# Low parts of w_down's weights: a ScalarE rounding with scale -1 and an accumulating DMA in place of VectorE's subtraction

## The chip, the cores and the metric

The kernel runs on one core of one Trainium2 chip. The metric is device microseconds of one execution: 2164.78 us in the median of 3 runs before the change (2164.6 to 2165.61).

## The reference, cut to what matters

Two layers of a streaming encoder are computed for a prompt of 512 frames and a sample of 64 frames with the same weights. Each layer has three kinds of attention over one combined projection, and then a gated feed-forward part:

```
xn = rmsnorm(x);  g, u = split(xn @ w_up)          # D_MODEL 1024, D_FF 2816
h  = gelu(causal_dwconv3(g)) * u
x  = x + h @ w_down                                # w_down: 2816 x 1024
```

All is float32. The kernel gets float32-like accuracy out of matmuls on operands of the shorter type fp32r: each factor is split into `hi` (the value rounded to fp32r) and `lo` (what the rounding left), and a product is the sum of three matmuls, hi\*hi, hi\*lo and lo\*hi. The change is about how `lo` of w_down's weights is made.

## The kernel before, in words

**Tokens.** Prompt and sample are handled together as 576 columns, in two halves of 288 (`halves`, L69), with the feature dimension on the partitions.

**Chunks.** All weights go through one list of *chunks* (`chunk`, L368), each of 128 rows by up to 1024 columns of float32 in SBUF. A chunk of w_in, w_up or w_out has eight k-tiles and one block of 128 output columns; a chunk of w_down has four k-tiles (two in the first group) and two column blocks (`ncol=2`). The main loop (`run_main`, L424) takes them in order. At the start of chunk i it asks for the weights of chunk i+2 (`fetch`, L375, a DMA from SP into `raw`, three buffers) and makes the generator `split(i + 1)` (L385) the first entry, label "w", of the list of pending steps. For each column block and each half it then issues the chunk's matmuls, k-tile by k-tile, in the order hi\*hi, hi\*lo, lo\*hi: the third matmul of a chunk is the first that reads `lo`. The results go to PSUM tiles from a pool of two (`pmm`); after each group VectorE adds or multiplies them out (`flush`, L411).

**split.** ScalarE rounds the two halves of `raw` to `hi`, and VectorE subtracts `hi` from `raw` to make `lo` (L400 to L406). `hi` and `lo` have two buffers each, so the tiles for chunk i+1 come free when PE has finished chunk i-1, which is the start of chunk i.

**Order.** There are no hand-written queues: a planner in the program (`charge`, `tick`) keeps a model clock for PE, ScalarE, VectorE and GpSimd, and lets each pending generator take its next step after every three matmuls, when the model says that its inputs are ready. "w" steps are first in the list and have no other condition. Each engine then runs what it got in that order. Only instructions issued through the wrapped engines (`scalar`, `vector`, `gpsimd`) are charged to the model clocks.

**Feed-forward part.** The 22 column blocks of w_up are taken in six groups (`FG`, L42: 2, 4, 4, 4, 4, 4). Block f has a gate chunk `g` (`evg`, L1247) and an up chunk `u` (`evu`, L1275), then `fin` (L1278): GpSimd multiplies `ge` by `ur`, ScalarE rounds the product to `hh`, VectorE subtracts to get `hl`. A group's part of w_down is a run of four chunks d0 to d3 (`down`, L1312); their evacuation (L1316) is VectorE's add of the PSUM tile `md` into `x`. The run for a group stands behind the `g` and `u` chunks of the next group's first block (of its last block for the last group), so `fin` of that block falls into the run's first chunk. In layer 0 the run of the last group follows directly and also starts the next norm for each finished tile (`norm_tile`, L507: ScalarE's `xhm` and square, VectorE's `xlm`, GpSimd's sum `accm`). In layer 1 the last group goes another way (`down_final`, L1327), with `half` set; it keeps the split as it was.

Of the kernel before, what the change touches and what calls it, by code (L numbers as in the profile page):

```python
# [13 lines left out]
AF = mybir.ActivationFunctionType  # L14
ALU = mybir.AluOpType
# [30 lines left out]
def trunk_kernel(ctx: ExitStack, tc: tile.TileContext, a: dict, o: dict):  # L46
    nc = tc.nc
# [15 lines left out]
    def slot(nm, dt=F32):  # L63
        return sp_.tile([P, TOK], dt, tag="s", name=nm, bufs=NS)
# [59 lines left out]
    scalar = Engine(nc.scalar, "ACT", act_cost)  # L124
# [260 lines left out]
    def split(i):  # L385

        c = chunks[i]
        if "hi" in c:
            return
        c["hi"] = None  # L390
        n = c["kt"] // 2
        raw = c["raw"]
        if c["half"] is None:
            hi, lo = (wp.tile(c["shape"], F32R, tag=f"w{t}", name=f"w{t}{c['nm']}", bufs=2) for t in ("hi", "lo"))
            hi, lo = ([t[:, 0:n, :], t[:, n:2 * n, :]] for t in (hi, lo))
        else:
            hi, lo = ([slot(f"w{t}{j}{c['nm']}", F32R)[:, 0:512].rearrange("p (k c) -> p k c", k=n)
                       for j in range(2)] for t in ("hi", "lo"))
        ks = slice(0, n), slice(n, 2 * n)
        scalar.copy(hi[0], raw[:, ks[0], :])  # L400
        t0 = cx["t"]
        scalar.copy(hi[1], raw[:, ks[1], :])
        cx["t"] = t0
        yield
        for j in range(2):
            vector.tensor_tensor(lo[j], raw[:, ks[j], :], hi[j].bitcast(F32), op=ALU.subtract)  # L406
        c["hi"], c["lo"] = ([t[k // n][:, k % n, :] for k in range(2 * n)] for t in (hi, lo))
# [16 lines left out]
    def run_main(start):  # L424
        for i in range(start, len(chunks)):
# [5 lines left out]
            if i + 1 < len(chunks):  # L431
                spawn("w", split(i + 1), True)
# [1146 lines left out]
    def split_first(i):  # L1579

        if i == 2:
            list(split(2))
            return w0.append((chunks[2]["hi"], chunks[2]["lo"]))
        raw = chunks[i]["raw"]
        hi, lo = ([slot(f"w{n}{i}{j}", F32R)[:, 0:512].rearrange("p (k c) -> p k c", c=P) for j in range(2)]
                  for n in "hl")
        for j in range(2):
            scalar.copy(hi[j], raw[:, 4 * j:4 * j + 4, :])
        for j in range(2):
            vector.tensor_tensor(lo[j], raw[:, 4 * j:4 * j + 4, :], hi[j].bitcast(F32), op=ALU.subtract)  # L1590
        w0.append(tuple([t[k // 4][:, k % 4, :] for k in range(ND)] for t in (hi, lo)))
        chunks[i]["raw"] = None
# [42 lines left out]
    for d in range(4, ND):  # L1635
        if d + 2 < ND:
            rows(d + 2)()
            square(d + 1)
        if d == 5:
            square(ND - 1)  # L1640
        if d == 6:
            list(split(3))
        for i in range(3):
            if d == 6 and i == 1:
                norm_end("m0")
            grow(i, d)
# [71 lines left out]
```

## Time and profile before

| | |
|---|---|
| median of 3 runs | 2164.78 us |
| the profiled execution's own time | 2164.78 us |
| its span, first to last instruction | 2163.0 us |
| PE matmul busy | 2135.8 us, 99% of the span |
| VectorE (DVE) busy | 1393.0 us, 64% |
| ScalarE (ACT) busy | 1041.3 us, 48% |
| GpSimd (POOL) busy | 398.1 us, 18% |
| 16 DMA engines, share taken by the SP queue | 30.6% |

How to read the rows: a timeline row is start in us, duration in us (of all the instructions that it merges), engine, line, operation, output and inputs, shape and count, and in brackets how long the engine was idle before it and for whom it waited. All instructions issued through the wrapped engines have line L102, so tiles tell them apart: `whid` and `wlod` are the hi and lo parts of a w_down chunk, `wrd` its raw weights. A waits row is who waited for whom: us in total, times, longest. A chain row is start, us, what. A grouped row ends in busy us, mean ns of one, and the idle time before. A DMA row ends in KB each and us from issue to landing, where that is known.

### The profile page before, as it was taken

The numbers are of one execution on the slowest core, as the hardware profiler recorded it, in microseconds if no ns is written. First come the engines' busy times: TensorE is split into PE (matmuls) and PEld (weight loads), VectorE is DVE, ScalarE is ACT, GpSimd is POOL, SyncE is SP. The second block draws the span as 40 slices with busy tenths as digits, with TensorE's granted clock in tenths as the row PEclk, the third lists the DMA queues.
The fourth block names the chain that finished last, engine by engine and source line by source line (L and its number), as shares of the span: only waits on it lengthen the run. The fifth ranks groups of instructions, "written<-read, shape, count | busy, mean of one in ns | idle before, by whom it ended". The sixth has DMA issues, their size and how long they took to land.

```text
span 2163.0 us, 39766 instructions
## 1 busy us (share of the span) xinstructions
PE 2135.8 (99%) x15911; PEld 2099.8 (97%) x15911; DVE 1393.0 (64%) x2860; ACT 1041.3 (48%) x2057; POOL 398.1 (18%) x523
## 2 busy tenths in 40 slices
PE   8999999999999999999999999999999999999998
PEld 7999999999999999999999999999999999999998
DVE  7886667767466655556678765667765566555564
ACT  5657776555434322323355677755554333222334
POOL 2111121111122111212110122201102112111221
PEclk9999999999999999999999999999999999999999
DMA  7442222223332322222243222233323322222222
GB/s 216 122 139 84 73 85 80 89 79 97 93 118 60 101 84 82 85 79 88 88 139 107 83 73 73 73 93 98 99 74 122 88 79 81 86 78 88 78 89 65
DMA packets 326563, 200.50 MB, mean 93 GB/s; under 512 B 10544, under 2 KB 320754, under 8 KB 326314
## 3 DMA queue, kind: packets, MB, share of 16 engines
q1 hardware_dynamic: 324618, 194.88, 30.6%
q0 software_dynamic: 1760, 3.08, 0.4%
q8 instruction: 125, 2.05, 0.4%
q14 instruction: 60, 0.49, 0.1%
HBM read 176.54 MB, written 25.83 MB: 94 GB/s over the span
## 4 chain that ended last, share of the span: by engine, by line
PE 92%; DVE 5%; issue 1%; ACT 1%; POOL 1%; DMA 0%; SPq 0%; DVEq 0%; POOLq 0%; ACTq 0%
PE md L131 11%; PE mg1f L131 6%; PE mg0f L131 6%; PE mu0f L131 6%; PE mu1f L131 6%; PE mo L131 4%; PE mg0a L131 2%; PE mg1a L131 2%; PE mg0b L131 2%; PE mg1b L131 2%; PE mg0c L131 2%; PE mg1c L131 2%; DVE wlod L102 1%; PE mb1a L131 1%; PE mb0a L131 1%
## 5 line engine op out<-in xcount | busy, mean ns | idle before, releaser
L102 DVE TENSOR_TENSOR x<-md,x 128x288 f32<-128x288 f32 x192 | 86.9, 455 | 117.2 <-PE md L131 116.3
L102 ACT CAST whid<-wrd 128x512 fp32r<-128x512 f32 (+1 forms) x88 | 46.8, 579 | 138.1 <-PE md L131 87.9
L131 PE MATMUL md<-hh0f,whid 128*128 128x288 f32 x352 | 104.9, 298 | 3.5 <-DVE x L102 3.5
L131 PE MATMUL mu0f<-xhf,wlou0f 128*128 128x288 f32 x352 | 103.8, 295 | 0.0
L131 PE MATMUL mu1f<-xhf,wlou1f 128*128 128x288 f32 x352 | 103.8, 295 | 0.0
L131 PE MATMUL md<-hh0f,wlod 128*128 128x288 f32 x352 | 103.8, 295 | 0.0
L131 PE MATMUL mg1f<-xhf,whig1f 128*128 128x288 f32 x352 | 103.7, 295 | 0.0
L131 PE MATMUL mg0f<-xhf,whig0f 128*128 128x288 f32 x352 | 103.7, 295 | 0.0
L131 PE MATMUL mg0f<-xhf,wlog0f 128*128 128x288 f32 x352 | 103.7, 295 | 0.0
L131 PE MATMUL mg1f<-xhf,wlog1f 128*128 128x288 f32 x352 | 103.7, 295 | 0.0
L131 PE MATMUL mu1f<-xlf,whiu1f 128*128 128x288 f32 x352 | 103.7, 295 | 0.0
L131 PE MATMUL mu0f<-xlf,whiu0f 128*128 128x288 f32 x352 | 103.7, 295 | 0.0
L131 PE MATMUL mu0f<-xhf,whiu0f 128*128 128x288 f32 x352 | 103.6, 294 | 0.0
L131 PE MATMUL mu1f<-xhf,whiu1f 128*128 128x288 f32 x352 | 103.6, 294 | 0.0
L131 PE MATMUL md<-hl0f,whid 128*128 128x288 f32 x352 | 103.6, 294 | 0.0
L131 PE MATMUL mg0f<-xlf,whig0f 128*128 128x288 f32 x352 | 103.6, 294 | 0.0
L131 PE MATMUL mg1f<-xlf,whig1f 128*128 128x288 f32 x352 | 103.6, 294 | 0.0
L131 PE MATMUL md<-hh1f,whid 128*128 128x288 f32 x288 | 85.7, 297 | 2.7 <-DVE x L102 2.7
L131 PE MATMUL md<-hh1f,wlod 128*128 128x288 f32 x288 | 84.9, 295 | 0.0
L131 PE MATMUL md<-hl1f,whid 128*128 128x288 f32 x288 | 84.8, 294 | 0.0
L131 PE MATMUL mo<-ml,whio 128*128 128x288 f32 x256 | 75.6, 295 | 0.8 <-DVE ml L102 0.8
L131 PE MATMUL mo<-mh,wloo 128*128 128x288 f32 x256 | 75.5, 295 | 0.0
(960 smaller groups left out, 8434.1 us busy)
## 6 DMA issues: line engine op xcount, KB each, us to landing
wrd<-in_w_down SPq DMA_DIRECT2D x40, 512.0 KB
wrg0f<-in_w_up SPq DMA_DIRECT2D x22, 512.0 KB
wru0f<-in_w_up SPq DMA_DIRECT2D x22, 512.0 KB
wrg1f<-in_w_up SPq DMA_DIRECT2D x22, 512.0 KB
wru1f<-in_w_up SPq DMA_DIRECT2D x22, 512.0 KB
wro<-in_w_out SPq DMA_DIRECT2D x16, 512.0 KB
xspill<-x SPq DMA_DIRECT2D x16, 288.0 KB
x<-xspill SPq DMA_DIRECT2D x16, 288.0 KB
```

The lines of the kernel that those rows point to most:

```text
L102: return f(*args, **kw)
L131: nc.tensor.matmul(out, lhsT=lhsT, rhs=rhs, start=start, stop=stop, skip_group_check=True)
```

## The change

For w_down chunks that have no `half`, ScalarE makes two more instructions: it writes the negated rounding of `raw` into the `lo` tile (a Copy with scale -1, output fp32r). Then one DMA issued from GpSimd adds `raw` into that tile (SBUF to SBUF, accumulating). VectorE's two subtractions of the chunk are gone, and `split` is done in one planner step, in which the DMA is charged to no model clock.

```diff
         if c["half"] is None:
             hi, lo = (wp.tile(c["shape"], F32R, tag=f"w{t}", name=f"w{t}{c['nm']}", bufs=2) for t in ("hi", "lo"))
+            c["lo_t"] = lo
             hi, lo = ([t[:, 0:n, :], t[:, n:2 * n, :]] for t in (hi, lo))
...
         scalar.copy(hi[0], raw[:, ks[0], :])
         t0 = cx["t"]
         scalar.copy(hi[1], raw[:, ks[1], :])
+        if c["nm"][0] == "d" and c["half"] is None:
+
+            for j in range(2):
+                scalar.activation(lo[j], raw[:, ks[j], :], AF.Copy, scale=-1.0)
+            nc.gpsimd.dma_start(c["lo_t"][:, 0:2 * n, :], raw, accum_op=ALU.add)
+            c["hi"], c["lo"] = ([t[k // n][:, k % n, :] for k in range(2 * n)] for t in (hi, lo))
+            yield
+            return
         cx["t"] = t0
         yield
         for j in range(2):
             vector.tensor_tensor(lo[j], raw[:, ks[j], :], hi[j].bitcast(F32), op=ALU.subtract)
```

## Rows read from the trace of the kernel before

**Rows 1.** The page: busy us, share of the span and instructions of each engine.
```profile
PE 2135.8 (99%) x15911; PEld 2099.8 (97%) x15911; DVE 1393.0 (64%) x2860; ACT 1041.3 (48%) x2057; POOL 398.1 (18%) x523
```
**Rows 2.** PE's waits over the whole span.
```profile
PE md L131 <- DVE x L102: 6.2, 15, 0.7
```
**Rows 3.** PE's waits in the stretches 690:760, 760:1040 and 1040:1095.
```profile
PE md L131 <- DVE x L102: 1.2, 2, 0.7
...
PE md L131 <- DVE x L102: 1.5, 4, 0.4
...
PE md L131 <- DVE x L102: 0.8, 3, 0.3
```
**Rows 4.** The chain that ended last, 744 to 800 us.
```profile
745.58 6.36 PE mu0f L131 x48
```
**Rows 5.** Timeline of PE, first matmul of a w_down run.
```profile
764.50 0.29 PE L131 MATMUL md<-hh0f,whid 128*128 128x288 f32 x1
```
**Rows 6.** Timeline of ScalarE: short run, ordinary run, layer 0's last run.
```profile
698.65 0.71 ACT L102 CAST whid<-wrd 128x256 fp32r<-128x256 f32 x2 [2.32 <-issue]
...
764.61 1.14 ACT L102 CAST whid<-wrd 128x512 fp32r<-128x512 f32 x2 [1.97 <-issue]
767.27 0.67 ACT L102 CAST hh0f<-ge0f 128x576 fp32r<-128x576 f32 x1 [1.52 <-POOL ge0f L102]
...
1067.93 1.12 ACT L102 CAST whid<-wrd 128x512 fp32r<-128x512 f32 x2
```
**Rows 7.** Timeline of VectorE: short run's end, ordinary run's start, layer 0's last run.
```profile
711.02 1.28 DVE L102 TENSOR_TENSOR wlog0f<-wrg0f,whig0f 128x512 fp32r<-128x512 f32 x2
...
765.26 2.53 DVE L102 TENSOR_TENSOR wlod<-wrd,whid 128x512 fp32r<-128x512 f32 x2
...
768.08 0.75 DVE L102 TENSOR_TENSOR hl0f<-ge0f,hh0f 128x576 fp32r<-128x576 f32 x1
768.74 0.45 DVE L102 TENSOR_TENSOR x<-md,x 128x288 f32<-128x288 f32 x1
...
1066.18 0.46 DVE L102 TENSOR_TENSOR x<-md,x 128x288 f32<-128x288 f32 x1 [0.68 <-PE md L131]
```
**Rows 8.** Timeline of GpSimd: short run's first chunk, ordinary run's first chunk.
```profile
699.38 1.43 POOL L102 TENSOR_TENSOR ge0f<-ge0f,ur0f 128x576 f32<-128x576 f32 x1 [6.15 <-ACT whid L102]
...
765.33 1.91 POOL L102 TENSOR_TENSOR ge0f<-ge0f,ur0f 128x576 f32<-128x576 f32 x1 [5.73 <-ACT whid L102]
```
**Rows 9.** Timeline of SP's queue in the same chunk.
```profile
767.82 0.37 SPq L383 DMA_DIRECT2D wrg0f<-in_w_up  x1
```
**Rows 10.** Groups by form, VectorE's subtractions for w_down.
```profile
L102 DVE TENSOR_TENSOR wlod<-wrd,whid 128x512 fp32r<-128x512 f32 x72 | 58.1, 849 | 2.4
L102 DVE TENSOR_TENSOR wlod<-wrd,whid 128x256 fp32r<-128x256 f32 x16 | 7.5, 512 | 0.0
```
**Rows 11.** Groups by form, ScalarE's casts and activations of 128x512.
```profile
L102 ACT CAST whid<-wrd 128x512 fp32r<-128x512 f32 x72 | 41.1, 618 | 119.4 <-PE md L131 79.8 <-issue 15.7 <-PE mg0f L131 11.9
...
L102 ACT ACTIVATE ge0f<-c0f 128x512 f32<-128x512 f32 x22 | 13.5, 615 | 0.0
```
**Rows 12.** DMA queues, and issues from GpSimd with KB and us to landing.
```profile
q1 hardware_dynamic: 324618, 194.88, 30.6%
...
ewin<-ebias POOLq DMA_DIRECT2D x1, 1536.0 KB, 12.8
...
out_sa_k<-in_cache_a_k POOLq DMA_DIRECT2D x2, 128.0 KB, 3.2
out_sa_v<-in_cache_a_v POOLq DMA_DIRECT2D x2, 128.0 KB, 4.4
```
**Rows 13.** Groups of GpSimd: what its DMA issues take of the engine.
```profile
L291 POOL DMA_DIRECT2D ewin<-ebias x2 | 2.3, 1133 | 11.0 <-DMA ebias<-ev 11.0
...
L363 POOL DMA_DIRECT2D out_sa_v<-in_cache_a_v x2 | 1.0, 498 | 0.0
```
**Rows 14.** Cores: span and mean granted clock.
```profile
core 0: 2163.0 us, clock 0.999
```

## The prediction

> **What bounds the kernel now.** I read the busy table first: PE is busy for 2135.8 of 2163.0 us and VectorE for 64% [rows 1]. So at most 27 us of PE's idle time could be won anywhere, and VectorE's load matters only where PE waits for it. The list of PE's waits puts a price on that: the w_down matmuls (tile `md`) wait 15 times for VectorE's add into `x`, 6.2 us in all [rows 2]. That is the ceiling of what taking work off VectorE here can return. By stretch it is 1.2 us around each layer's first, short w_down run (layer 1's line reads the same), 1.5 us in four waits, one for each ordinary run of layer 0, and 0.8 us in its last run [rows 3]; what is left for layer 1's ordinary runs is 6.2 - 2 x 1.2 - 1.5 - 0.8 = 1.5 us. Then I read how long a chunk lasts: 48 matmuls take 6.36 us of PE time, whether eight k-tiles by one column block or four by two [rows 4]. A first-group chunk (two k-tiles, 24 matmuls) is 3.18 us. Last I read, engine by engine, one chunk start and what hangs on it [rows 5 to 9].
>
> Call the start of a chunk T. In the run at 764.50 [rows 5], ScalarE begins to round the next chunk's weights at 764.61, when PE lets go of the two-deep `hi` buffer, and two casts take 1.14 us [rows 6]. VectorE's two subtractions follow at 765.26 and take 2.53 us [rows 7], so low parts that PE needs at T+6.36 are ready at T+3.3: three microseconds to spare.
>
> **The change, part by part.**
>
> *How often.* Only w_down chunks with no `half` are touched: the trace has 72 subtractions of 128x512 and 16 of 128x256 [rows 10], two a chunk, so 36 long chunks and 8 short ones, in runs of four: 9 long runs and 2 short ones. One long run is layer 0's last; the other eight and both short ones stand right behind an `up` chunk whose `fin` step (GpSimd's product, ScalarE's rounding to `hh`, VectorE's `hl`) shares the start of the run.
>
> *ScalarE.* Two more instructions a chunk. The trace has no Copy with a scale and no pointer here; the cast of 128x512 is 618 ns and the 128x512 activation 615 ns [rows 11], and pairs go through in 1.14 us, so I take 0.55 us more each: four end at T+2.3, in a short chunk (a pair is 0.71 us [rows 6]) at T+1.45. ScalarE is 48% busy, so the time itself is covered; only the chain counts.
>
> *VectorE.* 58.1 + 7.5 us of subtractions go [rows 10]. Off the path, but for the waits of rows 3. Of those 6.2 us I count back the eight of the ordinary runs (3.0), layer 0's last (0.8) and 0.5 at each short run's start, 4.8 us. The 0.7 at each short run's end follows the subtraction for the next gate chunk (711.02 [rows 7]), which stays.
>
> *The accumulating DMA.* No row shows one. From below: the quickest GpSimd DMA of the trace takes 3.2 us from issue to landing for 128 KB; from above: 12.8 us for 1536 KB [rows 12]. Between them: the SP queue's 194.88 MB held 30.6% of 16 engines [rows 12], 10590 engine-us over the span, so 512 KB needs 1.8 us of all sixteen and 128 KB 0.45. That makes 3.2 - 0.45 + 1.8 = 4.55 us for a copy, and 6.35 if reading the old value doubles the traffic. I take the middle, L = 5.5 us for 512 KB and 4.1 for 256 KB (issue and wake-up included), nearer the 128 KB row because it too stands alone on its queue; I keep 3.2 and 12.8 as ends.
>
> The Trainium skill ("DMA: Bandwidth & Descriptors", Anatomy of one DMA) gives 2.0 us plus bytes over 436 GB/s: by that 512 KB would land after an estimated 3.2 us. The trace's 128 KB DMAs took 3.2 and 4.4 us where that formula says 2.3. The skill's "Collectives: The Full Stack" (Part 3, why ReduceScatter is half of AllGather) says an add inside the DMA halves the rate because two sources are read; no run here shows it. Together they would make an estimated 4.4 us, and the sum below about 2183 us.
>
> *What the landing costs PE.* The low part is wanted by the third matmul, so weights must be there by T + 6.36 + 0.15 = T+6.5; they land at T+2.3+L. First chunk of a long run: 2.3+5.5-6.5 = 1.3 us late. The second chunk's chain starts when the first chunk starts, before that stall, so the stall is given back to it and it is on time; the third is late by 1.3 again, the fourth is not. L below 4.2 costs nothing. In a short run the chunk ahead is 3.18 us: need at T+3.3, landing at T+1.45+4.1 = 5.55, so second and fourth chunk are 2.2 us late each (the first follows a long chunk, need T+6.5, on time): 4.4 a run, 8.8 for two.
>
> *What is queued behind the DMA.* GpSimd is in order, and the DMA is emitted at the first planner step of a chunk, `fin`'s product at a later one. The product now starts at 765.33 = T+0.8 [rows 8]; it will wait for the fourth rounding (T+2.3) and for the issue (1.1 us, by the ewin issue's 1133 ns; the 64-row issues are 0.5 [rows 13]): T+3.45. Without the subtraction beside it, it runs 1.43 us, as at 699.38, not 1.91 [rows 8], to T+4.9. Then `hh` 0.67 (T+5.6) and `hl` 0.75 (T+6.35), and `hl` stands in VectorE's order ahead of the second add into `x` (768.08 before 768.74 [rows 7]). That add ends at T+6.8, but the fourth PSUM group of the chunk, which reuses its bank, wants to begin at T+4.77: PE waits 2.0 us. It overlaps the landing's 1.3 (both end at fixed times after T), so the first chunk costs 2.0, not 3.3. In short runs the same chain ends at T+6.0, inside the landing stall.
>
> *Layer 0's last run* has no `fin`, but its `xhm` and squares stand ahead of the roundings: the third chunk's first cast begins at 1067.93, while the add at 1066.18 shows its predecessor's start to be 1065.98 [rows 6, 7], so its chain is 1.9 us later than elsewhere. Cost: 1.3 at its first chunk, 2.3+1.9+5.5-6.5 = 3.2 at its third: 4.5.
>
> *SP's queue.* A weight fetch into the buffer that the DMA reads now waits for the landing (T+7.8) and not for the subtraction (767.82 = T+3.3 [rows 9]). That buffer is wanted for the rounding that starts three chunks on, at T+19, 11 us after the landing. The fetch is hidden behind those chunks and costs nothing; if that cover were gone, ScalarE's rounding, and with it the whole chain, would start later by what the fetch is late.
>
> *Clock.* 0.999 granted over the span [rows 14]; I count nothing for it, as the stalls are short.
>
> *Sum.* 8 x (2.0+1.3) + 4.5 + 8.8 - 4.8 = 26.4 + 4.5 + 8.8 - 4.8 = +34.9 us. The profiled execution took 2164.78 us, 1.8 more than its span and equal to the median of the runs: 2164.8 + 34.9 = 2199.7, say 2200 us.
>
> **Rivals.**
>
> *A, the transfer is hidden.* If L is 3.2 us (the 128 KB row taken as it stands; the DMA formula of the Trainium skill says the same), no long chunk waits for its landing. What is left: the product behind the DMA, 8 x 2.0; short runs 4 x (1.45+3.2-3.3) = 5.4; last run 0.9; less 4.8: +17.5, 2182 us. For it: the path is SBUF to SBUF. Against: four times the bytes and an add.
>
> *B, the transfer is slow.* With L = 8.5 (between 6.35 and the 12.8 row; other DMAs on the same engines, or a slower add): 4.3 late at two chunks of each long run, 8 x 8.6 = 69, last run 10.5, short runs 2 x 10.5, less 4.8: +95, 2260 us. At L = 12.8 it would be about +195. For it: the kernel's own fetches use the same engines. Against: they hold them for only 30.6%.
>
> *C, faster.* `fin`'s chain does not block: if the planner, with VectorE no longer charged, sets `hl` behind the second add, or the product ahead of the DMA, and L is under 4.2 us, then nothing is late in the long runs and the waits of rows 3 go: -4.8 in the ideal case, 2160 us. It decides where the product starts before T+1.6 or `hl` loses its place. Against: `split` is first in the list of steps, and the product's place depends on PE's and ScalarE's model clocks, which change little.
>
> **Numbers.** Forecast 0.50, A 0.19, B 0.22, C 0.05, no change to speak of 0.04. Predicted time 2200. The range runs from a little below A, 2176, to L = 8, 2250. A measurement of this kernel tells about 0.2%, 4.3 us, from no change: faster 0.05, same 0.04, slower 0.91; all of the forecast, A and B are slower.
>
> **What would show it.** In the profile after, PE's waits name the DMA into `wlod` (1 to 2 us, first and third chunk of long runs, second and fourth of short ones) and VectorE's `x` with about 2 us once in each run behind `fin`; GpSimd's product starts 2.6 us later in those chunks and lasts 1.4; VectorE loses some 65 us and ScalarE gains some 45. I am wrong if the DMA lands under 4 or over 8 us after its issue, if stalls come in every chunk and not every other, or if `hl` stands elsewhere.

## The result, and the profile after

The kernel after takes 2189.52 us in the median of 3 runs (2187.12 to 2189.56), the kernel before 2164.78: ratio 1.011, interval 1.0087 to 1.0133. That is 24.7 us slower, inside the range on record (2176 to 2250) and 10.5 us under the predicted 2200. The profiled execution's span grew from 2163.0 to 2187.3 us.

The page's first part answers to [rows 1]: VectorE has 62 us less, ScalarE 43 us more, and PE is busy 8.6 us longer for the same 15911 matmuls.

```profile
PE 2144.4 (98%) x15911; PEld 2105.2 (96%) x15911; DVE 1331.1 (61%) x2772; ACT 1084.3 (50%) x2145; POOL 425.1 (19%) x567
```

PE's waits over the whole span answer to [rows 2]. The adds into `x` went from 6.2 to 1.5 us, and a wait for the DMA into `wlod` stands in their place.

```profile
PE md L131 <- DMA wlod<-wrd: 15.0, 17, 2.5
PE md L131 <- ACT whid L102: 5.7, 9, 1.5
...
PE md L131 <- DVE x L102: 1.5, 4, 0.5
```

The second line I read as more of the first. The matmul that waits there is, all nine times, the third of its chunk, the first to read `wlod`, as in the row at 782.22 below; the `whid` cast that is running at that moment (781.48) fills the buffer of the next chunk.

The DMA part has the new queue's share and the landing, to set beside [rows 12]; the grouped rows have what one issue takes of GpSimd [rows 13] and one negated rounding of ScalarE [rows 11].

```profile
q0 software_dynamic: 8096, 24.05, 5.5%
...
wlod<-wrd POOLq DMA_DIRECT2D x36, 512.0 KB, 4.6
...
wlod<-wrd POOLq DMA_DIRECT2D x8, 256.0 KB, 3.4
```
```profile
L408 POOL DMA_DIRECT2D wlod<-wrd x44 | 37.8, 858 | 217.3 <-ACT wlod L102 167.8 <-PE md L131 33.9 <-DVE x L102 15.7
```
```profile
L102 ACT ACTIVATE wlod<-wrd 128x512 fp32r<-128x512 f32 x72 | 41.3, 621 | 0.0
```

The chain that ended last, around the first ordinary run of layer 0, is where the mechanism is read. The second low rounding ends at 763.85, the DMA is issued at 764.13, lands at 768.70, and PE goes on at 768.84.

```profile
762.69 1.16 ACT wlod L102 x2
763.85 0.29 issue
764.13 4.57 DMA wlod<-wrd
768.70 0.14 issue
768.84 7.38 PE md L131 x54
...
783.97 4.99 DMA wlod<-wrd
788.95 0.14 issue
789.09 6.34 PE md L131 x46
```

The timeline of PE shows the same run's start, T = 767.94 (764.50 in [rows 5]), and its three late chunks: the first, the third and the fourth. In brackets is the idle time before the row.

```profile
767.94 0.29 PE L131 MATMUL md<-hh0f,whid 128*128 128x288 f32 x1
...
768.84 0.37 PE L131 MATMUL md<-hh0f,wlod 128*128 128x288 f32 x1 [0.48 <-DMA wlod<-wrd]
...
782.22 0.37 PE L131 MATMUL md<-hh0f,wlod 128*128 128x288 f32 x1 [0.43 <-ACT whid L102]
...
789.09 0.37 PE L131 MATMUL md<-hh0f,wlod 128*128 128x288 f32 x1 [0.26 <-DMA wlod<-wrd]
```

Matmuls follow each other by 0.13 us, so the third of the first chunk was due at 768.20 and ran at 768.84: 0.64 late. Timelines of ScalarE, GpSimd and VectorE in that chunk answer to [rows 6 to 8].

```profile
768.05 1.14 ACT L102 CAST whid<-wrd 128x512 fp32r<-128x512 f32 x2 [0.26 <-ACT ge0f L102]
769.09 1.15 ACT L102 ACTIVATE wlod<-wrd 128x512 fp32r<-128x512 f32 x2
```
```profile
770.53 0.85 POOL L408 DMA_DIRECT2D wlod<-wrd  x1 [5.21 <-ACT wlod L102]
771.11 1.73 POOL L102 TENSOR_TENSOR ge0f<-ge0f,ur0f 128x576 f32<-128x576 f32 x1
```
```profile
770.43 0.46 DVE L102 TENSOR_TENSOR x<-md,x 128x288 f32<-128x288 f32 x1 [1.83 <-PE md L131]
772.02 0.46 DVE L102 TENSOR_TENSOR x<-md,x 128x288 f32<-128x288 f32 x1 [1.14 <-PE md L131]
773.58 0.76 DVE L102 TENSOR_TENSOR hl0f<-ge0f,hh0f 128x576 fp32r<-128x576 f32 x1 [1.10 <-ACT hh0f L102]
774.26 0.45 DVE L102 TENSOR_TENSOR x<-md,x 128x288 f32<-128x288 f32 x1
```

`hl` starts 5.6 us into the run (3.6 before), as forecast, but it now stands *behind* the second add into `x` (772.02), and no add waits for it.

Last, three stretches of 3.4 us were granted half the clock (1.2 of 2.4 GHz). The view by stretches has PE's granted clock before the last two figures (DMA share, GB/s):

```profile
704.40:707.70 3.30, 3.30 (x16) 3.30 (x15) 0.92 (x2) 0.00 (x0) 0.68 (x1) 0.50 0.95 228
1086.70:1090.00 3.30, 3.30 (x15) 3.30 (x15) 0.46 (x1) 0.59 (x2) 0.93 (x2) 0.50 0.74 186
1786.40:1789.70 3.30, 2.94 (x12) 2.97 (x13) 0.62 (x2) 0.00 (x0) 0.17 (x2) 0.50 0.91 180
```

Each came with one of PE's longest stalls, in the two short runs and in layer 0's last run (the timeline's idle times are 1.47, 2.07 and 2.51 us). The first two came right behind the stall; the third began before the stall ended, as the matmul that ends it already takes 0.58 us instead of 0.37. The fourth row is another long stall with none behind it, and so is a wait of 1.54 us later in the first short run.

```profile
703.11 0.37 PE L131 MATMUL md<-hh0f,wlod 128*128 128x288 f32 x1 [1.47 <-ACT whid L102]
...
1085.66 0.37 PE L131 MATMUL md<-hh0f,wlod 128*128 128x288 f32 x1 [2.07 <-DMA wlod<-wrd]
...
1786.76 0.58 PE L131 MATMUL md<-hh1f,wlod 128*128 128x288 f32 x1 [2.51 <-DMA wlod<-wrd]
...
1925.92 0.37 PE L131 MATMUL md<-hh1f,wlod 128*128 128x288 f32 x1 [1.70 <-DMA wlod<-wrd]
```

**Where the 24 us are.** From a run's first `md` matmul to the next chunk's first, seven ordinary runs took 26.08 us each before and 26.89 to 28.92 after, +10.4 in all. Layer 0's fourth ordinary run and last run together went from 53.20 to 58.74, +5.5 (2.1 and 3.4). The short runs went from 15.07 to 19.14 and 19.84, +8.8. That is 24.7 by these lengths and 24.3 by the span: the rest of the kernel did not move. Three stretches of 3.4 us at half clock lose some 1.7 us each (an estimate from their length), so about 5 of it is the clock: some 3.4 in the short runs, 1.7 in the last.

### The profile page after: what moved, and what is told of

Its sections match the earlier page's. It is cut to its first block, busy times and chain, and to the rows that moved or that the text cites. A ratio compares the mean times of both kernels' runs of the same rounds, so it can differ in the third digit from the quotient of the medians.

```text
span 2187.3 us, 39966 instructions
## 1 busy us (share of the span) xinstructions
PE 2144.4 (98%) x15911; PEld 2105.2 (96%) x15911; DVE 1331.1 (61%) x2772; ACT 1084.3 (50%) x2145; POOL 425.1 (19%) x567
## 4 chain that ended last, share of the span: by engine, by line
PE 58%; DMA 3%; issue 2%; ACT 2%; DVE 1%; POOL 0%; DVEq 0%; POOLq 0%; ACTq 0%
PE md L131 9%; PE mg1f L131 6%; PE mg0f L131 6%; PE mu1f L131 5%; PE mu0f L131 5%; DMA wlod<-wrd 3%; PE mg1a L131 2%; PE mg1b L131 2%; PE mg1c L131 2%; PE mo L131 2%; PE mb1a L131 1%; PE mv1b L131 1%; PE mv1a L131 1%; PE mv1c L131 1%; PE mk1a L131 1%
## 5 line engine op out<-in xcount | busy, mean ns | idle before, releaser
L131 PEld LDWEIGHTS md<-hh0f,wlod 128*128 128x128 f32 x352 | 67.3, 191 | 15.2 <-ACT whid L102 8.7
L408 POOL DMA_DIRECT2D wlod<-wrd x44 | 37.8, 858 | 217.3 <-ACT wlod L102 167.8
```

The costliest lines, as they stand in the source:

```text
L131: nc.tensor.matmul(out, lhsT=lhsT, rhs=rhs, start=start, stop=stop, skip_group_check=True)
L408: nc.gpsimd.dma_start(c["lo_t"][:, 0:2 * n, :], raw, accum_op=ALU.add)
```

## The experiments

Each edit is against the kernel after, unless another is named; `...` marks lines left out. Ratios are to the kernel before, run beside it.

**e1: the planner's charge.** Why did `hl` change its place? The two new ScalarE instructions are charged to the model clock; in e1 they go past the planner.

```diff
-                scalar.activation(lo[j], raw[:, ks[j], :], AF.Copy, scale=-1.0)
+                nc.scalar.activation(lo[j], raw[:, ks[j], :], AF.Copy, scale=-1.0)
```

> The changed kernel, but ScalarE's two new instructions are not charged to the planner's model clock, which puts VectorE's hl back ahead of the second add into x in the first chunk of the ordinary runs. Theory (the prediction's GpSimd chain is real, and only the order of VectorE hid it): product at T+3.2, hl ends at T+6.4, the second add at T+6.8, PE waits for VectorE's x about 1.3 us once in each of the 8 ordinary runs, on top of the DMA stalls: about +10 us over the changed kernel, 2200 us. Rival (the chain costs nothing, because the DMA's stall at the chunk's start covers it): 2189 to 2191 us and no new waits for x.

Measured: 2200.03 us, ratio 1.0161 (1.0147 to 1.0174), 10.5 us above the kernel after. VectorE's timeline has `hl` ahead of the second add again (which the third row merges with the one behind it); PE's has the wait, at the fourth PSUM group of the first chunk. Of the ten in PE's waits over the span, eight are such, one in each ordinary run:

```profile
770.77 0.46 DVE L102 TENSOR_TENSOR x<-md,x 128x288 f32<-128x288 f32 x1 [1.84 <-PE md L131]
773.91 0.76 DVE L102 TENSOR_TENSOR hl0f<-ge0f,hh0f 128x576 fp32r<-128x576 f32 x1 [2.68 <-ACT hh0f L102]
774.58 0.81 DVE L102 TENSOR_TENSOR x<-md,x 128x288 f32<-128x288 f32 x2
```
```profile
775.09 0.40 PE L131 MATMUL md<-hh0f,whid 128*128 128x288 f32 x1 [1.18 <-DVE x L102]
```
```profile
PE md L131 <- DMA wlod<-wrd: 12.6, 16, 2.1
PE md L131 <- DVE x L102: 10.1, 10, 1.8
```

So the chain that the prediction built on GpSimd exists and stalls PE as it said, if `hl` keeps its place. The charge moved `hl`, and that spares most of the 10.5 us: by their lengths the ordinary runs have 9.4 of it. The rest stands in layer 1's short run, which has one more stretch at half clock here.

**e2: the ceiling.** No low part is made for the touched chunks: `lo` is `hi`, and rounding, DMA and subtraction are gone.

```diff
-            for j in range(2):
-                scalar.activation(lo[j], raw[:, ks[j], :], AF.Copy, scale=-1.0)
-            nc.gpsimd.dma_start(c["lo_t"][:, 0:2 * n, :], raw, accum_op=ALU.add)
-            c["hi"], c["lo"] = ([t[k // n][:, k % n, :] for k in range(2 * n)] for t in (hi, lo))
+            c["hi"] = c["lo"] = [hi[k // n][:, k % n, :] for k in range(2 * n)]
```

> The two VectorE subtractions of each w_down chunk are dropped, and nothing takes their place: the low part of these weights is left out (PE multiplies with the high part a second time). This is the ceiling of what freeing VectorE can return. Theory: the waits behind the subtractions go (4.8 of 6.2 us), 2160 us, ratio 0.998. Rival (VectorE's waits only move to the next thing in its queue): 2164 us.

Measured: 2156.52 us, ratio 0.9961 (0.9949 to 0.9974): 8.6 us under the kernel before, nearly twice the 4.8 that I counted back. An ordinary run takes 25.44 us without a stall, so before it lost 0.64, while its one row of waits says 0.37 (1.5 us in four waits [rows 3]). A short wait of PE costs more here than the gap that the list shows.

**e3: the low part first.** The same instructions, with the two negated roundings and the DMA ahead of the two `hi` casts, so that the DMA starts about 1 us earlier. (The three lines taken out stand further down again, for the chunks that the change leaves alone.)

```diff
-        scalar.copy(hi[0], raw[:, ks[0], :])
-        t0 = cx["t"]
-        scalar.copy(hi[1], raw[:, ks[1], :])
         if c["nm"][0] == "d" and c["half"] is None:
...
             for j in range(2):
                 scalar.activation(lo[j], raw[:, ks[j], :], AF.Copy, scale=-1.0)
             nc.gpsimd.dma_start(c["lo_t"][:, 0:2 * n, :], raw, accum_op=ALU.add)
+            for j in range(2):
+                scalar.copy(hi[j], raw[:, ks[j], :])
```

> The changed kernel with the order of ScalarE's four instructions turned round: first the two negated roundings and the DMA, then the two high parts. The DMA is issued about 1.05 us earlier after each chunk start. Theory (PE's loss is the landing measured from the chunk start): landing at T+6.2 instead of T+7.3 against a need at T+6.5, so the ordinary runs lose nothing; short runs still 1.3 us late at two chunks each, last run of layer 0 about 1.6 us: 2165 to 2170 us. Rival (the loss is ScalarE's and GpSimd's longer work itself, or contention on the DMA engines): the same work is done, so within 5 us of the changed kernel's 2189.

Measured: 2176.01 us, ratio 1.0052 (1.0038 to 1.0065). The direction held (13.5 us under the kernel after); the size missed. In the run looked at above, which starts at T = 768.71 here, the rounding now goes first (ScalarE's timeline), its DMA is issued at T+1.65 instead of T+2.6 (GpSimd's), and the first and the third chunk are on time.

```profile
768.91 1.15 ACT L102 ACTIVATE wlod<-wrd 128x512 fp32r<-128x512 f32 x2 [0.34 <-PE mu0f L131]
```
```profile
770.36 0.85 POOL L404 DMA_DIRECT2D wlod<-wrd  x1 [5.18 <-ACT wlod L102]
```

But the landing is not constant. For the fourth chunk the DMA is issued as early, 1.7 us after the third chunk's start at 781.43, and takes 5.39 us instead of the median's 4.7; by the chain PE goes on at 788.56, 0.5 late:

```profile
783.13 5.39 DMA wlod<-wrd
788.51 0.04 issue
788.56 6.36 PE md L131 x46
```

Ordinary runs so took 25.44 to 26.97, the short ones 18.73 and 17.22, and layer 0's last run had a stall of 2.9 us, with 6.8 us at half clock that began in it. A third `lo` buffer, which would let the rounding start a chunk earlier, was not tried.

What makes one landing longer than another was not tried apart either, but the packets in the traces sort them. In the kernel after, 23 of the 36 transfers of 512 KB have no instruction fetch (a packet of 16 KB on queue q8) and at most 420 KB of SP's queue beside them, and these land in 4.47 to 4.65 us. Nine have an instruction fetch beside them and four have 480 to 512 KB of SP's queue; eleven of these 13 land in 4.99 to 5.87 us. The one behind the stall of 1.70 us at 1925.92 has an instruction fetch alone (the DMA part of 1920.01 to 1925.79):

```profile
q8 instruction: 1, 0.02, 1.0%
...
wlod<-wrd POOLq DMA_DIRECT2D x1, 512.0 KB, 5.8
```

In three of the four with SP's queue, the weight fetch had waited for the landing before (SP's waits name the DMA into `wlod` 40 times) and was issued some 0.05 us after it (1925.84 after 1925.79), so it ran beside the next adding DMA: a late landing can make the next one late.

**e4: two DMAs.** As e3, with a DMA of half the size behind each rounding (the edit is against e3).

```diff
                 scalar.activation(lo[j], raw[:, ks[j], :], AF.Copy, scale=-1.0)
-            nc.gpsimd.dma_start(c["lo_t"][:, 0:2 * n, :], raw, accum_op=ALU.add)
+                nc.gpsimd.dma_start(lo[j], raw[:, ks[j], :], accum_op=ALU.add)
```

> As the low-first kernel, but each half of the low part has its own accumulating DMA, issued right behind its rounding. Theory: the first half lands by T+4.5 and the second by T+5.6, against needs at T+6.5 and T+7.3; short runs late by 0.5 us at two chunks each; VectorE's waits gone: 2160 to 2165 us, at or just below the kernel before. Rival (a second issue of 0.86 us on GpSimd, in order, sets the pace): slower than the low-first kernel.

Measured: 2170.7 us (2169.08 to 2175.81), ratio 1.0029 (1.0018 to 1.0041); above what was expected. Seven ordinary runs are nearly whole (25.47 to 26.25), but layer 0's fourth takes 27.69, and the short ones 19.19 and 20.77: their longest stalls lose 2.1 and 2.5 us, with half clock beside them, here for 6.7 us in one row of the view by stretches. These lengths are of the slowest of the seven executions, 2175.81 us.

```profile
1783.10:1789.80 6.70, 6.23 (x24) 5.91 (x25) 2.68 (x6) 0.40 (x1) 0.00 (x0) 0.50 0.51 149
```

**e5: the price of the add.** The DMA copies instead of adding, over the same path and size; the low part then holds the whole weight.

```diff
-            nc.gpsimd.dma_start(c["lo_t"][:, 0:2 * n, :], raw, accum_op=ALU.add)
+            nc.gpsimd.dma_start(c["lo_t"][:, 0:2 * n, :], raw)
```

> The changed kernel with a plain copy in place of the accumulating DMA; the subtraction is left out, so the low part holds the whole weight. It prices the add in the DMA. Theory A (the add reads two sources and doubles the transfer, as in the prediction's upper figure): 512 KB lands about 1 us or more sooner, 3.6 us instead of 4.6 after the issue, and the kernel is at 2170 to 2176 us. Theory B (the add costs the transfer next to nothing, most of the 4.6 us is issue and completion): 4.3 to 4.6 us, 2185 to 2189 us.

Measured: 2168.09 us, ratio 1.0015 (1.0006 to 1.0024), 21.4 us under the kernel after. The DMA part beside that of the kernel after, and the row of its issues:

```profile
q0 software_dynamic: 8096, 24.05, 3.2%
...
wlod<-wrd POOLq DMA_DIRECT2D x36, 512.0 KB, 2.9
...
wlod<-wrd POOLq DMA_DIRECT2D x8, 256.0 KB, 2.5
```
```profile
L408 POOL DMA_DIRECT2D wlod<-wrd x44 | 24.7, 561 | 216.5 <-ACT wlod L102 199.8 <-DVE x L102 15.9 <-PE md L131 0.8
```

Landing 2.9 us against 4.6, issue 0.56 against 0.86, for the same bytes. Without the touched DMAs (e2) this queue has a share of 0.5%, so the adding DMAs hold the engines (5.5 - 0.5) / (3.2 - 0.5) = 1.85 times as long. Seven of the ordinary runs take 25.76 to 25.78 us, nearly without stalls, and one 26.33: 21.4 of the 24.7 us that the change loses go with the add, by its landing and its issue together. That is beyond theory A's 2170 to 2176, as the landing fell by 1.7 us and not by 1.

**e6 and e7: run by run.** e6 leaves the short chunks to VectorE, e7 layer 0's last run as well.

```diff
-        if c["nm"][0] == "d" and c["half"] is None:
+        if c["nm"][0] == "d" and c["half"] is None and n == 2:                             # e6
+        if c["nm"][0] == "d" and c["half"] is None and n == 2 and c["nm"][:4] != "d018":   # e7
```

> The changed kernel, but the eight short chunks (two k-tiles) keep VectorE's subtraction. Theory (the changed kernel's two short runs lost 4.1 and 4.8 us, part of it at half the granted clock): 8.8 us less than the changed kernel, 2180 to 2181 us, and one stretch at half clock left, in layer 0's last run. Rival (loss in proportion to the chunks touched, 8 of 44): 4.5 us less, 2185 us.

> As the one with the short chunks undone, and layer 0's last run keeps VectorE's subtraction as well; the eight ordinary runs alone are changed. Theory: another 3.4 us less, 2177 us, no stretch at half clock before the end, 1.2 to 2 us lost in each ordinary run. Rival (the clock falls after any run with stalls): stretches at half clock stay, 2180 us or more.

Measured: 2180.01 us, 1.0071 (1.0058 to 1.0085), and 2177.78, 1.006 (1.0046 to 1.0074). The short runs were worth 9.5 us, the last run 2.2, against the 8.8 and 3.4 read from the trace. In e7 the granted clock over the span is again that of the kernel before [rows 14], by the view of the cores:

```profile
core 0: 2175.0 us, clock 0.999
```

The 12.8 us that e7 still loses is the ordinary runs, now without help or harm from the clock.

**e8: both mends, ordinary runs only.** e4's order and halves with e7's condition (the edit is against e4).

```diff
-        if c["nm"][0] == "d" and c["half"] is None:
+        if c["nm"][0] == "d" and c["half"] is None and n == 2 and c["nm"][:4] != "d018":
```

> The two early half DMAs of the two-DMA kernel in the eight ordinary runs alone; short runs and layer 0's last run keep VectorE's subtraction. Theory: the landing is hidden in ordinary runs, which drop from 26.1 to 25.5 us each as in the kernel without low parts, and nothing else changes: 2160 to 2162 us, faster than both kernels (ratio 0.998). Rival (DMAs share engines with the weight fetches and now and then land late): 2163 to 2166 us, no difference.

Measured: 2163.54 us (2161.68 to 2164.95), ratio 0.9993 (0.9984 to 1.0002): no difference is told, and it is less than expected. Five of the eight runs take 25.5 to 25.7 us, but three take 26.57, 26.60 and (layer 0's fourth) 27.38. PE's waits:

```profile
PE md L131 <- DVE x L102: 3.3, 7, 0.7
PE md L131 <- DMA wlod<-wrd: 1.3, 6, 0.4
```

The seven waits for `x` stand at the runs that were left as before [rows 3]. Six waits for the DMA remain, and one transfer took 6.9 us to land.

**e9: only where it pays.** The one wait of an ordinary run for VectorE stands at one chunk, so only the low part of the second chunk (made while the first one runs) goes to the two DMAs (the edit is against e8).

```diff
-        if c["nm"][0] == "d" and c["half"] is None and n == 2 and c["nm"][:4] != "d018":
+        if c["nm"][0] == "d" and c["half"] is None and n == 2 and c["nm"][:4] != "d018" and c["nm"][-1] == "1":
```

> The two early half DMAs only where the kernel before shows VectorE's subtraction in PE's way: for the second chunk of each ordinary run, whose low part is made in the run's first chunk beside fin. All other low parts are VectorE's. Theory: 8 ordinary runs drop from 26.08 to about 25.5 us, 16 DMAs instead of 64 and none of them in a row, so none lands late: 2160 us, ratio 0.9975 to 0.998. Rival (the DMAs of the run's first chunk are the ones that GpSimd's order and the weight fetches delay): 2163 to 2165 us, no difference from before.

Measured: 2160.0 us (2159.59 to 2160.64), ratio 0.9979 (0.997 to 0.9988): 4.7 us faster than the kernel before, and the best of the complete kernels. The ordinary runs take 25.48 to 25.59, and of the waits of `md` only those of the untouched runs are left:

```profile
PE md L131 <- DVE x L102: 3.2, 7, 0.7
```

## Why the prediction was right, and where it was not

The sign, the place and the range were right; the largest term of the sum was nearly twice too large, and the two others met their size only with the clock's help, for which no term stood. Predicted terms are net of the waits counted back.

| term | predicted | measured |
|---|---|---|
| eight ordinary runs | 26.4 - 3.0 = +23.4 | +12.5 |
| layer 0's last run | 4.5 - 0.8 = +3.7 | +3.4, of which some 1.7 clock |
| two short runs | 8.8 - 1.0 = +7.8 | +8.8, of which some 3.4 clock |
| sum | +34.9 | +24.7 |

**Engine loads: right.** -62 and +43 us were measured where some -65 and +45 were said.

**The landing: right in form, a little too long.** By its own arithmetic, the weights land at T' + 2.2 + L (T' is the start of the chunk ahead) and are wanted at T' + 6.5. From the end of the last rounding to PE's matmul is 768.84 - 763.85 = 5.0 us, not 5.5, which makes 0.7 late; 0.64 was read. The plain copy that I bounded at 4.55 took 2.9, and the add, for which +1.8 was my upper end, cost +1.7 in landing: a copy end that was too high and the middle between copy and add cancelled in part, which is luck. The Trainium skill's formula ("DMA: Bandwidth & Descriptors", Anatomy of one DMA) gave an estimated 3.2 us for this copy, nearer than the 4.55 that I made of the 128 KB row, and its rule for ReduceScatter, that an add reads two sources and halves the rate ("Collectives: The Full Stack", Part 3), fits the 1.85; together they made an estimated 4.4 where 4.6 was measured. (With them the prediction's own sum comes to 2185, not to the 2183 that it says.)

**Every other chunk: half right.** The first chunk was late in all eight ordinary runs and the third in seven, as said, but five of them lose 0.4 to 1.3 us at the fourth too, and one loses 1.1 at the second. In the run shown, the third chunk starts at 781.37; its DMA is issued at 783.97, 2.6 us on, and takes 4.99 to land, longer than the median, so the low part is there 7.6 us after that start, 1.1 more than the 6.5 allowed. The stall of the third chunk (0.6) gives back only a part. I had one landing time for all; e3 shows 5.39 in the same place, and those with an instruction fetch or a whole weight fetch beside them were the long ones. The other runs differ in their places too: layer 0's last run stalls at its second and third chunk (first and third were said), layer 1's short run at its second and third (second and fourth).

**SP's queue: not quite nothing.** ScalarE never waits for a fetch into `wrd`, as said. But the fetch that now waits for a landing runs beside the next adding DMA (e3), which the prediction did not ask.

**GpSimd's chain: the step that failed.** "The first chunk costs 2.0" rested on "`hl` stands in VectorE's order ahead of the second add into `x`". The chain itself came as worked out: the product started at T+3.2 (3.45 said), and `hl` ended at T+6.4 (6.35 said). But `hl` was no longer ahead of that add. I read its place from the old trace, though that place is an output of the planner, and the change alters the planner's input: two charged ScalarE instructions ahead of `hh`. e1 takes the charge away and brings the old order and 10.5 us back. That `hl` stands elsewhere is one of the prediction's own signs of being wrong. Rival C named this condition too, and then dismissed it because the model clocks "change little". With L = 5.0 instead of under 4.2 it still was not faster.

**The clock: missing.** "I count nothing for it, as the stalls are short" cost about 5 us. The sum has stalls of 2.2 and 3.2 us in it, while the longest wait of `md` before was 0.7 [rows 2], so the clock of [rows 14] said nothing about them. That the stalls bring the half clock is read from their order in time and from its absence in e7's w_down runs, where the longest wait of `md` is 1.4 us. It was not measured by itself, and the row at 1925.92 shows that not each such stall does it.

**What VectorE gives back: too small.** 4.8 us was counted, 8.6 is there (e2), because I took the waits' rows as their price. The two waits of a short run were also taken the wrong way round: the one at the start is the longer, and it is the other that stays in e2. The timeline of PE before has them:

```profile
701.85 0.41 PE L131 MATMUL md<-hh0f,whid 128*128 128x288 f32 x1 [0.74 <-DVE x L102]
...
712.72 0.40 PE L131 MATMUL md<-hh0f,whid 128*128 128x288 f32 x1 [0.51 <-DVE x L102]
```

The transfer's stalls ate it all.

**The rivals.** A's 2182 lies nearer the result (7.5 us) than my 2200 (10.5), but for the wrong reason: its transfer was hidden and its GpSimd chain stalled, and on the chip it was the other way round. B is out, with a landing of 4.6 us and not 8.5.

## What to carry to other kernels

Before you move work to a slower path, compare its latency with the slack of the one it replaces: the subtractions were ready three microseconds early, and the adding DMA was some 0.6 us late in an ordinary run's first chunk and made stalls of 1.5 to 2.5 us in the short ones. Where a planner writes the order of the engines, an instruction's place in the old trace is no constant of the kernel: ask what the change charges to the planner. And move only what is waited for; with two early halves, one chunk in four of the ordinary runs (e9) gave 4.7 us where all the touched chunks (e4) cost 5.6.

## What the runs showed of the hardware

An adding DMA of 512 KB from SBUF to SBUF lands 4.6 us after its issue in the median and a copying one after 2.9; at 256 KB it is 3.4 and 2.5; and the issue holds GpSimd for 0.86 us instead of 0.56. Two adding DMAs of 256 KB, issued one behind the other, take 4.4 us each in the median (e4), so halving the size buys little where the next half follows at once: in e9 seven of the eight pairs have nothing else beside them, and there the first lands after 3.3 to 3.4 us and the second after 4.3. Adding DMAs of 512 KB land later, after 5.0 to 5.9 us, in eleven of 13 cases with an instruction fetch or 480 KB and more of SP's queue beside them (kernel after). PE's half clock came with single stalls whose idle rows say 1.47, 2.07 and 2.51 us, and stayed for 3.4 us (6.7 in e4); behind stalls of 1.54 and 1.70 us it did not come.
